# The opening of an encoder layer: 1/rms spread without a diagonal, chunk 0 by halves, the last squares summed apart, sums of h behind plain weights

## Chip, core and metric

The kernel runs on one core of a Trainium2 chip. The metric is the device time of one execution, in microseconds (us), as the median of several runs. TensorE (PE, with its weight loads PEld), VectorE (DVE), ScalarE (ACT), GpSimd (POOL) and SyncE (SP) run their own queues and wait for each other by semaphores; SP, ACT and POOL also issue DMAs.

## The reference

One layer on x (512 tokens, 1024 columns), all in float32, conditioned by a vector c:

```
mod = silu(c) @ w_mod + b_mod            # nine vectors: shift, scale, gate for three blocks
h = rmsnorm(x, norm_ffn1) * (1 + sc1) + sh1
x = x + 0.5 * g1 * swiglu(h, w_ffn1_in, w_ffn1_out)
h = rmsnorm(x, norm_mix) * (1 + sc2) + sh2
x = x + g2 * (merged(window attention, differential attention of h @ w_in) @ w_out)
h = rmsnorm(x, norm_ffn2) * (1 + sc3) + sh3
x = x + 0.5 * g3 * swiglu(h, w_ffn2_in, w_ffn2_out)
```

`rmsnorm(x, g)` is `x / sqrt(mean(x*x) + 1e-6) * g`, and `swiglu` is `(silu(gate) * up) @ w_out` with 2816 hidden columns.

## The kernel before

x lies transposed: 8 chunks of 128 model columns on the partitions, 512 tokens along the row. Products are made from two float32r parts of each operand, a high part (a cast on ACT, L185) and a low part (the difference on DVE, L186), as three products: high by high, high by low, low by high (`mm3`, L173 to L176).

**The opening** (from L606) is written out in the order in which each engine runs it (`manual_schedule`). c is loaded as one row and spread over the partitions by two products with a row of ones (L609); ACT takes SiLU of it into `cact`. While x arrives, ACT squares each chunk (DVE one of them, chunk 5), DVE adds the squares up, and PE sums them over the partitions with a column of ones (`Norm.sums`, L337), which leaves the sum for token t on partition t. DVE scales it (L307), POOL takes the power -0.5 (L308). To bring 1/rms of the tokens from the partitions onto the row of every partition, DVE multiplies the identity with it into a diagonal (`diagonal`, L316) and PE multiplies ones by that diagonal into a PSUM bank (`spread`, L329). `warm` (L615) puts products of the identity into PE's queue in between; their result is not used.

Then the 8 chunks follow. Of each chunk's scale and shift vectors DVE makes the column by multiplying a 128 x 1024 slice of w_mod with `cact` and summing the row (`mod_col`, L272), and for the scale a second, one-column operation applies the norm's gain (L279). `hidden` (L342) then makes h of the chunk: DVE x * scale * 1/rms (L346), ACT adds the shift into the high part (L347) and once more into a copy `value` (L350), DVE the low part (L351). PE multiplies the chunk by a 128 x 768 slice of weights, 18 products of 512 tokens into six banks (L689): three pairs of gate and up columns (q = 0, 1, 2). The weights' low parts are made by DVE for even chunks (L639), and for odd chunks by a negation on ACT (L632) and an adding DMA from POOL (L633). SP loads w_mod into the six slots of the tile `u` (4096 bytes a partition each) and weights into the four slots of `raw`; a load waits until its slot is free, and SP issues in order.

**The plain tiles** (from L835) come next, q = 3, 4, 5: each takes two loads of 128 x 1024 weights, splits them into parts and makes 48 products. `finish` (L723) reads a tile's pair of banks: SiLU on ACT (L725), the product on DVE (L726), and a split. Here PE, DVE and ACT are ordered by the scheduler of the tile framework, by its own cost model, with what is written first preferred; SP and POOL are in the order written. So DVE and ACT instructions of this part may stand ahead of instructions of the opening in their queue. **The sums of h** (`h_sum`, L587) subtract copies of h (L574, L576) and split the result into the operands n1, n2, t3, t4, which the later units of the first FFN multiply (a Strassen-like scheme: `Unit`, `two`, L444 to L446, 256 tokens each); n1 lies in slots of `u`. The first of them is read after q = 5.

Two **boundaries** later in the kernel (`boundary` at L360, and the one before the second FFN from L1752 on) repeat the norm on halves of the tokens (`HALVES`, T1 and T2), with `close`, `diagonal` and `spread` placed by step numbers among PE's products.

The pool lays out SBUF tile by tile in the order of first use, all slots of a tile side by side: the small tiles, ones, ident, then u (first used for c's row), par, x, the high and low parts with small columns between, ka, b, raw, f.

Of the kernel before, what the change touches and what calls it, by code (L numbers as in the profile page):

```python
# [11 lines left out]
F32 = mybir.dt.float32  # L12
# [122 lines left out]
def layer(ctx: ExitStack, tc: tile.TileContext, a: dict):  # L135
# [48 lines left out]
    def split_from(hi, lo, src):  # L184
        S.copy(hi, src)  # L185
        V.tensor_tensor(lo, src, f(hi), ALU.subtract)  # L186


    turn, holders = [0], {}

# [75 lines left out]

    def mod_col(v, c, w=None, in_order=False):
# [4 lines left out]
        ins = V.tensor_tensor_reduce(  # L272
            out=w, in0=w, in1=cact[0], scale=by, scalar=0.0 if v in norms else b, op0=ALU.mult, op1=ALU.add,
            accum_out=t,
        )
        if in_order:
            tc.keep_in_program_order(ins)
        if v in norms:
            V.scalar_tensor_tensor(t, t, par[:, norms[v] + c : norms[v] + c + 1], b, ALU.mult, ALU.add)  # L279

    class Norm:
# [28 lines left out]

        def diagonal(self, rs, r=FULL[0]):

            n = r.stop - r.start
            nt = n // P
            diag = f2()[:, 0:n]
            V.tensor_tensor(  # L316
                diag.rearrange("p (t q) -> p t q", t=nt),
                ident.unsqueeze(1).broadcast_to([P, nt, P]),
                rs.unsqueeze(2).broadcast_to([P, nt, P]),
                ALU.mult,  # L320
            )
            return diag

        def spread(self, diag, r=FULL[0]):

            n = r.stop - r.start
            rb = self.st[r.start] if n < T else bank("op")
            rb = rb[:, T - n : T]
            PE.matmul(rb, ones, diag, start=True, stop=True)  # L329
            return rb  # L330
# [11 lines left out]
    def hidden(rb, c, sc, sh, hi, lo, r=FULL[0], value=None):  # L342

        t = f2()[:, r]
        s = modv[sh][:, c : c + 1]
        V.scalar_tensor_tensor(t, x[c][:, r], modv[sc][:, c : c + 1], rb, ALU.mult, ALU.mult)  # L346
        S.activation(hi[:, r], t, AF.Identity, bias=s)  # L347
        yield
        if value is not None:
            S.activation(value, t.rearrange("p (t q) -> p t q", t=2), AF.Identity, bias=s)  # L350
        V.scalar_tensor_tensor(lo[:, r], t, s, f(hi[:, r]), ALU.add, ALU.subtract)  # L351
        yield
# [7 lines left out]
    def boundary(parts, g, norm, sc, sh, hh, hl, into, ahead, at):  # L360
# [29 lines left out]
        with tc.manual_schedule(engines=BOUND):  # L390
# [5 lines left out]
            for m, products in parts:  # L396
                po = bank("sc")[:, 0 : 2 * P]
                for _ in products(po, rb):
                    n += 1
                    if n == at[0]:  # L400
                        diag = norm.diagonal(norm.close(ra), ra)
                    elif n == at[1]:
                        ha = h_steps(norm.spread(diag, ra), ra)
                        run(ha, at[4])
# [5 lines left out]
            run(ha, at[6])  # L410
            diag = norm.diagonal(rs, rb)
            run(ha)
            run(steps, at[3])
            hb = h_steps(norm.spread(diag, rb), rb)
            run(hb)
# [189 lines left out]

    with tc.manual_schedule(engines=BOUND | {mybir.EngineType.SP, mybir.EngineType.Pool}):  # L606
        cb = [bank("sc") for i in range(2)]
        for i in range(2):
            PE.matmul(cb[i], ones[0:1, :], crow[:, i * T : (i + 1) * T], start=True, stop=True)  # L609

        def warm(n):

            out = bank("sc")[:, 0:P]
            for i in range(n):
                PE.matmul(out, ident, ident, start=True, stop=True)  # L615

        warm(8)
        w1 = {}

        def first_loads(k):  # L620
            scale = mod_load(SC1, k)
            raw = sbuf("raw", [P, 1024], F32, RAW)
            nc.sync.dma_start(raw[:, 0:768], a["w1s"][k])
            w1[k] = scale, mod_load(SH1, k), raw

# [19 lines left out]
        for c in range(NC):  # L645
            sq = f2()
            if c == 5:
                V.tensor_tensor(sq, x[c], x[c], ALU.mult)
            else:
                S.activation(sq, x[c], AF.Square)  # L650
            if c:
                V.tensor_tensor(sq, sq, before, ALU.add)
# [4 lines left out]
        n1.sums(sq, FULL[0], True, True)  # L657
        mod_col(SC1, 0, w1[0][0])
        rs = n1.rstd(FULL[0])
        warm(6)  # L660
        diag = n1.diagonal(rs)
        rb1 = n1.spread(diag)
        warm(5)
        mod_col(SH1, 0, w1[0][1])
        out1 = [b for _ in range(3) for b in pair_banks()]
        first_split(0)
        for k in range(NC):
            if k % 4 == 0:
# [3 lines left out]
                values = values.rearrange("p (t k q) -> p t k q", t=2, k=4)  # L672
            h1 = hidden(rb1, k, SC1, SH1, hh[k], hl[k], value=values[:, :, k % 4, :])
            next(h1)
            if k + 3 < NC:
                first_loads(k + 3)
            if k == 0:
                first_split(1)
                first_low(0)
            elif k + 1 < NC:  # L680
                mod_col(SC1, k + 1, w1[k + 1][0])
            next(h1)
            if k == 0:
                mod_col(SC1, 1, w1[1][0])
            wh, wl = w1.pop(k)[3:]
# [149 lines left out]
    with tc.manual_schedule(engines={mybir.EngineType.SP, mybir.EngineType.Pool}):  # L835
        for q in range(3):
            finish(q, out1[2 * q : 2 * q + 2])
        sums1 = ["n1", "n2", "t3", "t4"]
        units1 = {p: in_unit1(p) for p in range(PLAIN, NH)}
        for q in range(3, 2 * PLAIN):  # L840

            w = loaded1 or [load_split(a["w1i"][q - 3, k], aside=ASIDE * (q == 5)) for k in range(2)]
            loaded1 = None
            out = pair_banks()
            for k in range(NC):
                wh, wl = w[k // 4]
                for i in range(2):
                    o = (k % 4) * 256 + i * P
                    mm3(out[i], wh[:, o : o + P], wl[:, o : o + P], hh[k], hl[k], k == 0, k == NC - 1)
            for _ in range(2):  # L850
                if sums1:
                    h_sum(sums1.pop(0))
            finish(q, out)
            if q == 3:
# [890 lines left out]
    with tc.manual_schedule(engines=BOUND):  # L1745
# [28 lines left out]
        for q in ("a12", "a22"):  # L1774
            plain.prepare(q)
        diag = n3.diagonal(rs, T2)
        run(ha)
        lead.prepare("a12")
        run(steps, at[3])
        hb = h_steps(n3.spread(diag, T2), 1)  # L1780
        run(hb, 3)
# [95 lines left out]
def lay_out(i):  # L1877
# [4 lines left out]
    o["x"] = con(n["x"].reshape(T, NC, P).transpose(1, 2, 0))  # L1882
    o["c"] = n["c"].reshape(D)
    o["pos"] = con(n["positions"].reshape(NT, P).T)
# [54 lines left out]
```

## Time and profile before

| | us |
|---|---|
| median of 3 runs | 1062.57 |
| lowest and highest | 1062.09, 1063.57 |
| profiled execution, its own time | 1061.53 |
| its span, first to last instruction | 1059.8 |
| PE busy | 1040.5 |
| DVE busy | 794.8 |
| ACT busy | 566.2 |

In the rows of the timeline a start and a duration in us come first, then engine, line, operation, what is written and read by tile name, the count of merged instructions, and in brackets the idle time before and what ended it. A group's row has its busy time, the mean of one in ns, and the idle time before. A float32 product shows as two records, a float32r product as one; records of products that follow each other overlap.

### The profile page before, as it was taken

To read this page: it belongs to the slowest core of one execution; us is meant where nothing else is said; L and a number is where in the kernel's file an instruction comes from. 1 tells how busy PE (TensorE), PEld (TensorE's weight loads), DVE (VectorE), ACT (ScalarE), POOL (GpSimd) and SP (SyncE) were. 2 spreads that over 40 slices of the span, in tenths; PEclk is the share of its full clock that TensorE was granted. 3 is DMA by queue.
4 is the path that set the end of the run, shared out by engine and by line. 5 is a ranking of instruction groups with operands and counts; after the bars stand their busy time and mean duration, and the time that the engine had idled before them with its cause. 6 is when DMAs were issued, how large, how long until landed. Compare 5 with 4: busy or idle time off the path is not lost.

```text
span 1059.8 us, 18652 instructions
## 1 busy us (share of the span) xinstructions
PE 1040.5 (98%) x7316; PEld 952.6 (90%) x7316; DVE 794.8 (75%) x1459; ACT 566.2 (53%) x928; POOL 154.9 (15%) x174
## 2 busy tenths in 40 slices
PE   7999999999999999999999999999999999999998
PEld 5789889899899998899778778989999999999997
DVE  7985667667796679859773587977889787867867
ACT  5564334344454352667765755534766546655553
POOL 1100010100110100443211101001111211112210
PEclk9999999999999999999999999999999999999999
DMA  9968687966974459695747843975498998988974
GB/s 340 365 208 201 209 212 190 265 158 203 281 184 152 165 199 410 217 269 126 180 92 186 225 148 101 371 224 118 97 232 195 222 230 215 222 221 214 214 151 125
DMA packets 69082, 220.91 MB, mean 208 GB/s; under 512 B 8193, under 2 KB 10881, under 8 KB 68994
## 3 DMA queue, kind: packets, MB, share of 16 engines
q1 hardware_dynamic: 46512, 146.52, 38.6%
q0 software_dynamic: 19488, 68.70, 35.2%
q10 hardware_dynamic: 2994, 4.51, 1.2%
q8 instruction: 57, 0.93, 0.3%
q14 instruction: 31, 0.25, 0.1%
HBM read 209.46 MB, written 10.23 MB: 207 GB/s over the span
## 4 chain that ended last, share of the span: by engine, by line
PE 78%; DVE 8%; issue 5%; ACT 5%; DMA 2%; POOL 1%; SPq 0%; ACTq 0%; DVEq 0%; POOLq 0%
PE acc L446 5%; PE acc L444 5%; PE acc L445 5%; PE sc L174 5%; PE sc L446 5%; PE sc L444 5%; PE sc L175 5%; PE sc L445 5%; PE sc L176 5%; PE acc L174 4%; PE acc L175 4%; PE acc L176 4%; PE acc L1045 2%; PE acc L1047 2%; PE acc L1046 2%
## 5 line engine op out<-in xcount | busy, mean ns | idle before, releaser
L185 ACT CAST high<-raw 128x1024 fp32r<-128x1024 f32 (+2 forms) x162 | 158.3, 986 | 166.6 <-PE acc L445 39.1
L186 DVE TENSOR_TENSOR low<-raw,high 128x1024 fp32r<-128x1024 f32 (+2 forms) x162 | 183.6, 1141 | 59.4 <-ACT high L185 58.5
L444 PE MATMUL acc<-b,high 128*128 128x256 f32 x508 | 141.0, 278 | 0.3 <-DVE f L523 0.3
L445 PE MATMUL acc<-b,high 128*128 128x256 f32 x508 | 140.6, 277 | 0.1
L446 PE MATMUL acc<-b,low 128*128 128x256 f32 x508 | 140.6, 277 | 0.0
L444 PE MATMUL sc<-b,high 128*128 128x256 f32 x500 | 138.4, 277 | 1.4 <-ACT f L521 1.4
L446 PE MATMUL sc<-b,low 128*128 128x256 f32 x500 | 138.5, 277 | 0.0
L445 PE MATMUL sc<-b,high 128*128 128x256 f32 x500 | 138.4, 277 | 0.0
L186 DVE TENSOR_TENSOR low<-u,high 128x1024 fp32r<-128x1024 f32 (+1 forms) x73 | 87.5, 1200 | 27.6 <-ACT high L185 26.2
L185 ACT CAST high<-u 128x1024 fp32r<-128x1024 f32 (+1 forms) x73 | 75.5, 1035 | 54.8 <-PE sc L175 16.0
L174 PE MATMUL sc<-b,high 128*128 128x512 f32 (+1 forms) x280 | 100.8, 360 | 0.0
L175 PE MATMUL sc<-b,high 128*128 128x512 f32 (+1 forms) x280 | 100.3, 358 | 0.0
L176 PE MATMUL sc<-b,low 128*128 128x512 f32 (+1 forms) x280 | 100.2, 358 | 0.0
L444 PEld LDWEIGHTS acc<-b,high 128*128 128x128 f32 x508 | 95.4, 188 | 0.8 <-DVE f L523 0.5
L445 PEld LDWEIGHTS acc<-b,high 128*128 128x128 f32 x508 | 95.5, 188 | 0.4 <-DVE b L1727 0.3
L446 PEld LDWEIGHTS acc<-b,low 128*128 128x128 f32 x508 | 95.4, 188 | 0.2 <-DVE low L186 0.2
L444 PEld LDWEIGHTS sc<-b,high 128*128 128x128 f32 x500 | 94.0, 188 | 1.6 <-ACT f L521 1.6
L446 PEld LDWEIGHTS sc<-b,low 128*128 128x128 f32 x500 | 93.9, 188 | 0.3 <-DVE low L186 0.2
L445 PEld LDWEIGHTS sc<-b,high 128*128 128x128 f32 x500 | 93.9, 188 | 0.0
L174 PE MATMUL acc<-b,high 128*128 128x512 f32 (+1 forms) x248 | 92.1, 371 | 0.2 <-DVE u L186 0.2
L176 PE MATMUL acc<-b,low 128*128 128x512 f32 (+1 forms) x248 | 90.2, 364 | 0.0
L175 PE MATMUL acc<-b,high 128*128 128x512 f32 (+1 forms) x248 | 90.1, 363 | 0.0
(369 smaller groups left out, 2675.4 us busy)
## 6 DMA issues: line engine op xcount, KB each, us to landing
u<-w_mod SPq DMA_DIRECT2D x40, 512.0 KB, 7.8
b<-w_mod SPq DMA_DIRECT2D x32, 512.0 KB, 6.0
raw<-w2i SPq DMA_DIRECT2D x31, 512.0 KB, 5.5
u<-w2i POOLq DMA_DIRECT2D x31, 512.0 KB, 7.0
u<-w1u POOLq DMA_DIRECT2D x24, 512.0 KB, 7.1
raw<-w1u SPq DMA_DIRECT2D x24, 512.0 KB, 6.8
raw<-w1o SPq DMA_DIRECT2D x24, 384.0 KB, 4.2
raw<-w_gate SPq DMA_DIRECT2D x16, 512.0 KB, 5.6
```

Source lines behind the costliest of these rows:

```text
L174: PE.matmul(out, wh, xh, start=first, stop=False)
L175: PE.matmul(out, wh, xl, start=False, stop=False)
L176: PE.matmul(out, wl, xh, start=False, stop=last)
L185: S.copy(hi, src)
L186: V.tensor_tensor(lo, src, f(hi), ALU.subtract)
L444: PE.matmul(out, wh[:, s], xh, start=first and j == 0, stop=False, skip_group_check=True)
L445: PE.matmul(out, wh[:, s], xl, start=False, stop=False, skip_group_check=True)
L446: PE.matmul(out, wl[:, s], xh, start=False, stop=last and j == 1, skip_group_check=True)
L1045: PE.matmul(out[t][:, 0:n], hh[k][:, ht], wh[:, o : o + n], start=k == 0, stop=False)
L1046: PE.matmul(out[t][:, 0:n], hh[k][:, ht], wl[:, o : o + n], start=False, stop=False)
L1047: PE.matmul(out[t][:, 0:n], hl[k][:, ht], wh[:, o : o + n], start=False, stop=k == NC - 1)
```

## The change

It has six parts.

1. 1/rms is spread by products of its column, broadcast along the row as the stationary operand, with the identity as the moving one, 128 tokens each; `diagonal` goes, here and at both boundaries. c is loaded as eight columns and spread in the same way, so it takes a slot of the small tiles and none of u.
2. All squares are made on ACT. The sum runs over the first seven, and the last one is summed over the partitions by products of its own.
3. Chunk 0's h is made in two halves of 256 tokens.
4. The one-column operation for the scale (L279) moves from DVE to ACT for chunks 1 to 7. For chunk 0 the shift's slice is loaded ahead of the weights, and its column is made ahead of the spread.
5. The warm-up products are placed anew, some with chunks of x as the moving operand.
6. The next plain tile's loads and splits are written out ahead of the products of the one before, each behind the splits before them; the sums of h and `finish` are held behind splits of plain weights (`issue_after`), and all of n2, t3, t4 come with q = 5.

As u is now used first after b, its slots lie behind b's; every other tile keeps its place within 4096 bytes.

```diff
     def split_from(hi, lo, src):
-        S.copy(hi, src)
-        V.tensor_tensor(lo, src, f(hi), ALU.subtract)
+        last = S.copy(hi, src), V.tensor_tensor(lo, src, f(hi), ALU.subtract)
+        split[:] = [i.ins for i in last]
...
-    crow = u4(F32).rearrange("p a b -> p (a b)")[0:1, :]
-    nc.scalar.dma_start(crow, a["c"].unsqueeze(0))
+    ccol = small(NC)
+    nc.scalar.dma_start(ccol, a["c"])
...
         if v in norms:
-            V.scalar_tensor_tensor(t, t, par[:, norms[v] + c : norms[v] + c + 1], b, ALU.mult, ALU.add)
+            if beside:
+                S.activation(t, t, AF.Identity, bias=b, scale=par[:, norms[v] + c : norms[v] + c + 1])
+            else:
+                V.scalar_tensor_tensor(t, t, par[:, norms[v] + c : norms[v] + c + 1], b, ALU.mult, ALU.add)
...
-        def spread(self, diag, r=FULL[0]):
+        def spread(self, rs, r=FULL[0]):
...
-            PE.matmul(rb, ones, diag, start=True, stop=True)
+            for t in range(n // P):
+                PE.matmul(
+                    rb[:, t * P : (t + 1) * P], rs[:, t : t + 1].broadcast_to([P, P]), ident,
+                    start=t == 0, stop=(t + 1) * P == n, skip_group_check=True,
+                )
...
+        warm(4)
         cb = [bank("sc") for i in range(2)]
-        for i in range(2):
-            PE.matmul(cb[i], ones[0:1, :], crow[:, i * T : (i + 1) * T], start=True, stop=True)
...
-        warm(8)
+        for n in range(NC):
+            i, j = n // 4, n % 4
+            PE.matmul(
+                cb[i][:, j * P : (j + 1) * P], ccol[:, n : n + 1].broadcast_to([P, P]), ident,
+                start=j == 0, stop=j == 3, skip_group_check=True,
+            )
+        warm(5)
...
             sq = f2()
-            if c == 5:
-                V.tensor_tensor(sq, x[c], x[c], ALU.mult)
-            else:
-                S.activation(sq, x[c], AF.Square)
-            if c:
+            S.activation(sq, x[c], AF.Square)
+            if c == NC - 1:
+                last = sq
+            elif c:
                 V.tensor_tensor(sq, sq, before, ALU.add)
...
+                warm(4, x[c + 1])
+            elif c > 4:
+                warm(3, x[c])
+            if c == NC - 2:
+                n1.sums(sq, FULL[0], True, False)
+        n1.sums(last, FULL[0], False, True)
         mod_col(SC1, 0, w1[0][0])
         rs = n1.rstd(FULL[0])
-        warm(6)
-        diag = n1.diagonal(rs)
-        rb1 = n1.spread(diag)
         warm(5)
         mod_col(SH1, 0, w1[0][1])
+        rb1 = n1.spread(rs)
+        warm(4)
...
+            if k == 0:
+                h1 = [
+                    hidden(rb1, k, SC1, SH1, hh[k], hl[k], r, values[:, i : i + 1, k, :]) for i, r in enumerate(HALVES)
+                ]
...
-                mod_col(SC1, k + 1, w1[k + 1][0])
-            next(h1)
+                mod_col(SC1, k + 1, w1[k + 1][0], beside=True)
+            for h in h1:
+                next(h)
...
-            w = loaded1 or [load_split(a["w1i"][q - 3, k], aside=ASIDE * (q == 5)) for k in range(2)]
-            loaded1 = None
+            w, sums_from = loaded1, split[1]
+            if q < 5:
+                with tc.issue_after(split[0]), tc.issue_after(split[1]):
+                    loaded1 = [load_split(a["w1i"][q - 2, k], aside=ASIDE * (q == 4)) for k in range(2)]
+            behind = split[1]
...
-            for _ in range(2):
-                if sums1:
-                    h_sum(sums1.pop(0))
-            finish(q, out)
+            if q != 4:
+                with tc.issue_after(sums_from):
+                    for t in ("n1",) if q == 3 else ("n2", "t3", "t4"):
+                        h_sum(t)
+            with tc.issue_after(behind):
+                finish(q, out)
...
-                diag = n3.diagonal(n3.close(T1), T1)
+                rsa = n3.close(T1)
             elif i == len(last) - 1:
                 run(steps, at[1])
-                ha = h_steps(n3.spread(diag, T1), 0)
+                ha = h_steps(n3.spread(rsa, T1), 0)
```

On the host, c is laid out as 128 rows of 8 instead of one row of 1024.

More of the change, by code (lines that the diff above doesn't have):

```diff
@@ L349, in hidden @@
         if value is not None:
-            S.activation(value, t.rearrange("p (t q) -> p t q", t=2), AF.Identity, bias=s)
+            if r.stop - r.start == T:
+                t3 = t.rearrange("p (t q) -> p t q", t=2)
+            else:
+                t3 = t.unsqueeze(1)
+            S.activation(value, t3, AF.Identity, bias=s)
         V.scalar_tensor_tensor(lo[:, r], t, s, f(hi[:, r]), ALU.add, ALU.subtract)
@@ L606, in layer, with warm @@
     with tc.manual_schedule(engines=BOUND | {mybir.EngineType.SP, mybir.EngineType.Pool}):
-        cb = [bank("sc") for i in range(2)]
-        for i in range(2):
-            PE.matmul(cb[i], ones[0:1, :], crow[:, i * T : (i + 1) * T], start=True, stop=True)
[L611 to L615, printed above, removed]
-        warm(8)
+        fill = bank("acc")[:, 0:P]
+        def warm(n, by=ident):
+            for i in range(n):
+                PE.matmul(fill, ident, by[:, 0:P], start=True, stop=True)
+        warm(4)
+        cb = [bank("sc") for i in range(2)]
+        for n in range(NC):
[5 more added lines that the diff above has]
+        warm(5)
         w1 = {}
```

45 lines of the change are left out of this document (18 added, 27 removed).

## The prediction

> **What bounds the kernel now.** The page first, for the engine that fills the span, then the busy time by stretches of 10 us, then the order of time in the stretch where that engine is not full.
>
> ```profile
> span 1059.8 us, 18652 instructions
> PE 1040.5 (98%) x7316; PEld 952.6 (90%) x7316; DVE 794.8 (75%) x1459; ACT 566.2 (53%) x928; POOL 154.9 (15%) x174
> ```
>
> PE is the bound, with 19 us idle, and even those 98% hold warm-up products. So the time can fall in two ways: useful products begin sooner or follow each other without holes, or a product takes less.
>
> ```profile
> 10.00:20.00 10.00, 7.37 (x39) 6.19 (x38) 8.03 (x14) 3.16 (x5) 1.04 (x1) 0.83 1.03 411
> 20.00:30.00 10.00, 8.31 (x36) 6.19 (x35) 9.93 (x19) 6.51 (x10) 1.79 (x2) 1.00 1.01 346
> 30.00:40.00 10.00, 9.87 (x43) 7.70 (x42) 9.96 (x18) 5.55 (x8) 0.86 (x1) 1.00 1.04 373
> 40.00:50.00 10.00, 9.38 (x39) 6.77 (x38) 10.00 (x18) 4.65 (x7) 1.71 (x2) 1.00 1.05 356
> 50.00:60.00 10.00, 10.00 (x46) 8.25 (x45) 9.90 (x17) 8.08 (x14) 0.00 (x0) 1.00 0.94 291
> ```
>
> Columns: PE, PEld, DVE, ACT, POOL busy, granted clock, DMA share, GB/s. From 20 to 50 DVE is full and PE is not; but DMA is full too, from 10 to 50. That second saturation decides how much of a DVE saving can be cashed. From 50 on PE is full. Now the head of the stretch in order of time:
>
> ```profile
> 9.17 1.26 ACT L650 ACTIVATE f<-x 128x512 f32<-128x512 f32 x2 [0.58 <-DMA x<-x]
> 9.95 2.28 DVE L652 TENSOR_TENSOR f<-f,f 128x512 f32<-128x512 f32 x3
> 12.29 1.09 PE L337 MATMUL tp<-ones,f 128*128 128x2 f32 x8 [2.15 <-DVE f L652]
> 13.79 1.04 POOL L308 TENSOR_TENSOR sm<-sm,half 128x4 f32<-128x4 f32 x1 [4.75 <-DVE sm L307]
> 14.86 0.69 DVE L316 TENSOR_TENSOR f<-ident,sm 128x512 f32<-128x512 f32 x1 [1.16 <-POOL sm L308]
> 15.94 1.35 PE L329 MATMUL op<-f,ones 128*128 128x512 f32 x2
> 17.32 0.75 DVE L346 SCALAR_TENSOR_TENSOR f<-x,mod,op 128x512 f32<-128x512 f32 x1 [0.57 <-PE op L329]
> 18.88 0.50 PE L689 MATMUL acc<-b,high 128*128 128x512 f32 x1 [0.48 <-ACT b L347]
> 54.28 0.39 PE L689 MATMUL acc<-b,high 128*128 128x512 f32 x1
> ...
> 56.09 0.39 PE L174 MATMUL acc<-b,high 128*128 128x512 f32 x1
> ```
>
> The 144 products of L689 (8 chunks of 18) run from 18.88 until the plain tile q=3 begins at 56.09: 37.2 us. Between the last two rows lie 8 starts in 1.81 us, 0.227 each, so 144 need 32.7. The opening is 18.9 us of waiting and 4.5 us of holes. That is the store from which most parts of the change can draw.
>
> **The change part by part.** *Last squares apart.* Squares 6 and 7 wait for x (9.17), so they end at 10.4 as before. Adds shrink from three after 9.95 to two that can begin at 9.4 (square 5 is now ACT's), spacing 0.80, so the sum of seven ends near 10.9 instead of 12.2. But PE then has the sums of seven (8 records, 1.09), three warm-ups queued behind x[7] (6 records of about 0.11) and the sums of the last square: 10.95 + 0.9 + 0.7 + 1.1 = 13.6, against 13.4 now. I put this at 0; the ends are -0.7 (warm-ups not in the way) and +1.0 (if the clock is low).
>
> *Spread without a diagonal.* L316 goes: from POOL's end at 14.83 PE starts at once, 4 products of 2 records. The clock row says 0.83 for 10 to 20, so the two records of 1.35 us were partly at the low clock; 8 records of 0.11 to 0.21 plus 0.16 of drain are 1.05 to 1.85. At the high clock, which denser warm-ups should hold, the spread ends at 15.9, L346 starts at 15.95 instead of 17.32: -1.4 (at the low clock -0.6).
>
> *Chunk 0 by halves.* Two multiply-adds and two activations on 256 columns, where a pair on 512 took 1.56 (17.32 to 18.88); half-size ones overlap, so the first product is about 0.1 sooner: near 17.4, -1.5. DVE pays about 0.4 for four short instructions and for waiting on the activations before the low parts (an estimate), so chunk 1 gains only 1.0.
>
> *DVE's rounds.* In this stretch:
>
> ```profile
> L272 DVE CUSTOM_DVE_ANT_0 u<-u,ka,par 128x1024 f32<-128x1024 f32 x7 | 8.9, 1277 | 0.0
> L279 DVE SCALAR_TENSOR_TENSOR mod<-mod,par,begin 128x1 f32<-128x1 f32 x7 | 1.5, 214 | 0.1
> L576 DVE TENSOR_TENSOR b<-b 128x512 f32<-128x512 f32 x2 | 1.4, 684 | 0.0
> L186 DVE TENSOR_TENSOR u<-b,u 128x512 fp32r<-128x512 f32 x2 | 1.4, 684 | 0.0
> ```
>
> L279 moves to ACT (7 x 0.21), the sums of h (2 x L576, 2 x L186) leave the stretch: 1.5 + 2.8 = 4.3 us of DVE in the rounds, about the 4.5 us of holes. On ACT the small activation stands ahead of the copy of h, of the next cast of a weight and of its negation, whose POOL transfer waits for it; ACT is busy 5 to 6 of 10 us there, and the wait for L272 (1.2) falls where it now idles. I cost it at 0; without that cover up to 0.3 a round. The shift for chunk 0 is issued one load sooner and the first weight one later (some 1.3 us, to 13.4); its cast (0.8) still ends before 15.9. The column load of c has 128 short rows instead of 1 and its 8 products against ident may leave SiLU late; that sits behind the x that squares 6 and 7 wait for (9.17), and up to 0.5 us of it is hidden there.
>
> *What is late next: loads.* DVE would now let PE run unbroken from chunk 1, but odd chunks take their low weights by transfer:
>
> ```profile
> 28.01 0.50 PE L689 MATMUL acc<-b,low 128*128 128x512 f32 x1 [1.30 <-DMA low<-w1s]
> 34.65 0.84 ACT L630 CAST high<-raw 128x768 fp32r<-128x768 f32 x1 [1.21 <-DMA raw<-w1s]
> 36.52 0.86 POOL L633 DMA_DIRECT2D low<-w1s  x1 [9.63 <-ACT low L632]
> low<-w1s POOLq DMA_DIRECT2D x4, 384.0 KB, 7.8
> raw<-w1i SPq DMA_DIRECT2D x6, 512.0 KB, 9.1
> ```
>
> Chunk 1's transfer is issued some 1.4 sooner, as the activations ahead of its negation on ACT end that much sooner, and releases PE near 26.5 instead of 28.0. Unbroken PE would then want chunk 5's low part at 26.5 + 6 x 0.227 + (3 x 18 + 12) x 0.227 = 42.9. Its raw weight is DMA-bound (ACT waited for it at 34.65), and 36.52 + 7.8 = 44.3 is where it lands now. With DMA full before and after, a sooner request buys at most what idles; I take 43.4, between 42.4 and 44.3. After it PE has 6 + 36 products: 43.4 + 9.5 + 0.1 = 53.0. The opening ends 3.0 us sooner (2.0 to 4.0); losing the early start to a low clock would not change this end, since the loads set it.
>
> *Sums behind plain weights.* Work moves past PE's full stretch from 50 on, where only the due time counts: n1 by the first unit after q=5, the others 8 us later, with the casts of q=4 and q=5 now written out ahead of the products of the tile before. On SP the two w1i loads of the next tile now stand ahead of the first unit's load and a column's load, which are due 30 us later; POOL's adding transfer for that unit follows them and has the same room. I cost all this at 0, and its bad end is the last rival.
>
> *The moved tile.* c no longer takes a slot of u before everything else, so the pool lays the six slots of u behind b: they began 32 bytes off the 64-byte grid on which b, high and low lie, and come to lie on it. PE's groups by tile:
>
> ```profile
> L445 PE MATMUL sc<-b,high 128*128 128x256 f32 x500 | 138.4, 277 | 0.0
> L445 PE MATMUL sc<-u,high 128*128 128x256 f32 x72 | 20.1, 280 | 0.0
> L444 PE MATMUL acc<-u,high x80: 277/279/281, 100.1 to 1006.1; 128*128 128x256 f32 x80
> L174 PE MATMUL acc<-b,u 128*128 128x256 f32 x48 | 13.7, 286 | 0.0
> ```
>
> The same operation takes 277 ns in the mean with b moving and 280 with u. These records overlap, and a product that is 3 ns longer holds up the next by as much. (80 + 72) x 3 lines = 456 products x 3 ns = 1.4 us gained; 48 x 3 = 144 with u as weights (and b moving) may lose as much each, 0.4. I take -1.0, between -1.8 (456 x 4 ns, from 281, the longest of a row, to 277) and +0.4 (only the loss is real). The Trainium skill speaks against this term: SBUF — State Buffer, "Who interferes with whom", says that PE never waits on any other reader, and TensorE: Matmul & The Clock Gate, "Part 2: What happens when you issue a matmul", that loading weights takes no read bandwidth from the running product. By these an address changes nothing and the sum is 1.0 smaller; the rows above differ by tile, so I keep the term.
>
> *Later boundaries.* The diagonal also goes at both boundaries:
>
> ```profile
> 738.17 2.36 DVE L186 TENSOR_TENSOR low<-raw,high 128x1024 fp32r<-128x1024 f32 x2 [1.18 <-ACT high L185]
> 740.45 0.42 DVE L316 TENSOR_TENSOR f<-ident,sm 128x256 f32<-128x256 f32 x1
> 740.92 0.70 PE L329 MATMUL op<-f,ones 128*128 128x256 f32 x2 [0.50 <-DVE f L316]
> ```
>
> Here it stood behind two low parts and PE waited 0.5 for it. PE then waits again for DVE's next low part, which comes 0.3 sooner: -0.3 (0 to -0.5). Elsewhere PE does not wait for a diagonal.
>
> Sum: -3.0 - 1.0 - 0.3 = -4.3 us. The profiled execution took 1061.5 (span 1059.8), 1.0 below the median of 1062.57, so 1057.2 for it and 1058.3 for the median; the ends give -6.3 to -1.6.
>
> **The rivals.** *The address is worth nothing*: 1062.57 - 3.3 = 1059.3. For: 3 ns are 1% of a record whose end is modelled, and slot and bank differ between the groups too; against: it differs at the same line, with the same form, to the same bank.
>
> *The gain is given back to a load in the first FFN.*
>
> ```profile
> 172.45 1.05 ACT L185 CAST high<-raw 128x1024 fp32r<-128x1024 f32 x1 [3.82 <-DMA raw<-w1u]
> 140.00:150.00 10.00, 10.00 (x50) 8.40 (x49) 6.04 (x9) 1.05 (x1) 0.87 (x1) 1.00 0.60 193
> 150.00:160.00 10.00, 10.00 (x90) 10.00 (x88) 6.40 (x7) 6.02 (x7) 1.72 (x2) 1.00 1.04 292
> ```
>
> ACT stands 3.8 us for this load, with the copy that frees PE's bank behind it, and DMA is full (1.04) from 150 to 160. If the load keeps its time, the stall swallows the opening's 3.0: 1062.57 - 1.3 = 1061.3. Against: DMA is at 0.60 before 150, so the requests are released by engines, which come sooner too.
>
> *Casts of q=4 ahead of the finishing of q=0 (slower).* The load splits are now written out early; if ACT's order puts both casts before the SiLU that frees q=3's banks, PE at q=3 waits for a load.
>
> ```profile
> 44.13 2.11 SPq L211 DMA_DIRECT2D raw<-w1i  x2
> L725 ACT ACTIVATE f<-acc 128x512 f32<-128x512 f32 x3 | 1.6, 599 | 0.9 <-PE acc L689 0.9
> L726 DVE TENSOR_TENSOR f<-f,sc 128x512 f32<-128x512 f32 x3 | 1.9, 682 | 0.1
> ```
>
> The second request at 45.9 lands at 45.9 + 9.1 = 55.0; cast, SiLU, product: 55.0 + 1.05 (the cast at 172.45) + 0.6 + 0.7 + 0.5 for the handoffs between the two engines (an estimate) = 57.9, 1.8 after today's 56.09: 1062.57 + 1.8 - 1.3 = 1063.1 (a little slower); with DVE's two low parts (2.4) ahead of the product as well, 1065.5. It decides once that load lands after 51.0 or so. Against: the loads now go out ahead of others on SP, and the finishing of q=0 is written out first.
>
> **How the numbers follow.** Forecast 0.66, address worthless 0.12, swallowed 0.12, slower order 0.10. A change of under 0.2% (2.1 us) can't be told from none. Faster: 0.63 of the forecast's 0.66, 0.10 of the second; slower: half of the last and a little: 0.73, 0.20, 0.07. The forecast's own range is 1056.3 to 1061.0; to hold 8 in 10 with both later cases, 1055.6 to 1062.6.
>
> **What would show it.** Right: first L689 near 17.4, L174 of q=3 near 53.0, PE's longest hole in between before a low part by transfer and none before L347; no L576 in the rounds; u and b moving at one mean; PE's wait at the second boundary's spread gone; the clock at 1.00 from 13 to 17. Wrong: q=3 starting after 55, a hole between 53 and 90, or the stall near 174 longer by the same amount.

## The result, and the profile after

The changed kernel takes 1081.84 us (median of 6 runs, 1077.55 to 1083.53) against 1063.94 for the kernel before in the same series: a ratio of 1.0162, 95% interval 1.0137 to 1.0187. That is 17.9 us slower. The forecast was 1058.3, with 1055.6 to 1062.6 as its range.

The profiled execution of after took 1083.53 us (span 1081.6, before 1059.8), which is 22.0 more than the profiled one of before; the medians lie 17.9 apart. The head of its page:

```profile
span 1081.6 us, 18770 instructions
PE 1061.4 (98%) x7374; PEld 975.8 (90%) x7374; DVE 792.0 (73%) x1447; ACT 570.3 (53%) x938; POOL 156.1 (14%) x174
```

PE's busy time grew by 20.9 us and its idle time by only 0.9, though the change gives it only 58 records more, all of them small. So most of the loss is not waiting: PE takes longer over the same products. To find where, take the same product in both traces and subtract its start before from its start after:

| the product that starts before at | 60 | 120 | 160 | 180 | 240 | 320 | 500 | 540 | 740 | 760 | 860 | 960 | 1040 |
|---|---|---|---|---|---|---|---|---|---|---|---|---|---|
| after is later by, us | 0.6 | 1.4 | 1.6 | 0.5 | 1.4 | 3.0 | 3.5 | 11.3 | 11.4 | 12.6 | 15.6 | 19.0 | 21.8 |

There are two slow rises, one in each FFN (60 to 340 and 760 to 1040), and one leap between 500 and 540, in the attention, of which the diff touches no line. The 1.2 between 740 and 760 come with a stretch of half clock (755.8 to 759.2 in the clock's record). The opening gives 0.6 of loss instead of 3.0 of gain.

*The rises.* Busy time by stretches of 50 us in the second FFN, first before, then after (the count behind PE is that of its products):

```profile
800.00:850.00 50.00, 50.00 (x443) 50.00 (x442) 40.98 (x62) 30.80 (x48) 9.62 (x11) 1.00 0.91 210
850.00:900.00 50.00, 50.00 (x441) 50.00 (x440) 37.90 (x56) 27.67 (x40) 9.57 (x11) 1.00 0.92 223
```

```profile
800.00:850.00 50.00, 50.00 (x427) 50.00 (x426) 43.66 (x69) 31.51 (x52) 8.70 (x10) 1.00 0.88 212
850.00:900.00 50.00, 50.00 (x427) 50.00 (x426) 36.29 (x50) 24.58 (x32) 8.72 (x10) 1.00 0.91 213
```

PE is full and its clock 1.00 in all four rows, but it gets through 427 products where it got through 442. The groups by tile say of which kind they are, after:

```profile
L445 PE MATMUL sc<-b,high x500: 276/281/281, 92.6 to 1076.6; 128*128 128x256 f32 x167
L444 PE MATMUL acc<-u,high x80: 281/281/281, 100.9 to 1026.7; 128*128 128x256 f32 x80
```

and the first of these before:

```profile
L445 PE MATMUL sc<-b,high x500: 276/276/287, 92.0 to 1054.9; 128*128 128x256 f32 x167
```

(shortest, median and longest record in ns.) The median product with b moving went from 276 to 281. Those with u moving, which the change put on the 64-byte grid, did not fall to 276: they stand at 281, as against 279 before. One unit item of 24 products with u moving and the 120 products with b behind it, before and after, by windows cut at their first products:

```profile
100.06:102.86 2.80, 2.80 (x26) 2.80 (x25) 2.80 (x4) 1.73 (x3) 0.00 (x0) 1.00 1.01 349
102.86:116.48 13.62, 13.62 (x123) 13.62 (x121) 8.60 (x14) 6.18 (x9) 0.00 (x0) 1.00 0.40 126
```

```profile
100.94:103.76 2.82, 2.82 (x26) 2.82 (x25) 2.67 (x4) 2.82 (x5) 0.00 (x0) 1.00 0.77 236
103.76:117.89 14.13, 14.13 (x122) 14.13 (x121) 10.07 (x15) 6.29 (x10) 0.86 (x1) 1.00 0.51 133
```

The counts include a product or two carried over from ahead of the cut. Start to start, u's 24 take 2.80 and 2.82 us, the same. The 120 behind them take 13.62 (113.5 ns each) before and 14.13 (117.8) after, though operands, weights, banks and lines are the same and lie at the same offsets modulo 4096. From the start times one sees two paces and hardly anything between them: 113.3 ns and 117.8. Of the units' products with b moving (the b products) 92% (first FFN) and 88% (second) are under 115.5 ns before, 5% and 6% after. The pace hardly depends on what DVE or ACT do beside it: grouped by the instruction that runs there, the means after lie between 117.0 and 117.8 in every group of 50 products or more.

*The leap.* The chain of waits in the attention, after (start, us, what), and the stretch from 530 to 540 by windows, before and after:

```profile
525.11 0.96 ACT low L1005
526.07 0.46 issue
526.53 8.23 DMA low<-w_gate
534.80 0.79 PE acc L176
```

```profile
530.00:540.00 10.00, 9.58 (x65) 7.77 (x64) 7.15 (x20) 7.01 (x19) 1.71 (x2) 1.00 0.58 131
```

```profile
530.00:540.00 10.00, 5.57 (x14) 4.12 (x13) 3.56 (x12) 4.01 (x13) 1.96 (x2) 0.70 0.72 145
```

PE waits 4.4 us for a gate's low part, and the granted clock drops behind the wait (0.70 in the mean; half from 533.9 to 540.8 in the clock's record), which costs another 3.4. That transfer is not later than the rest of the stage, as its issue before and after shows:

```profile
522.87 0.91 POOL L986 DMA_DIRECT2D low<-w_gate  x1 [6.30 <-ACT low L985]
```

```profile
526.53 0.91 POOL L1006 DMA_DIRECT2D low<-w_gate  x1 [6.47 <-ACT low L1005]
```

It goes out 3.66 us later, where all else is 3.5 later. The instructions are those of before, but PE's order in this stage is another one, and it comes to this gate's products sooner.

*The opening*, in order of time:

```profile
8.63 0.60 ACT L661 ACTIVATE ka<-sc 128x512 f32<-128x512 f32 x1 [0.93 <-PE sc L618]
9.12 2.18 ACT L653 ACTIVATE f<-x 128x512 f32<-128x512 f32 x4
9.78 2.28 DVE L657 TENSOR_TENSOR f<-f,f 128x512 f32<-128x512 f32 x3 [2.00 <-ACT f L653]
14.85 1.27 DVE L273 CUSTOM_DVE_ANT_0 u<-u,ka,par 128x1024 f32<-128x1024 f32 x1
15.03 2.00 POOL L312 TENSOR_TENSOR sm<-sm,half 128x4 f32<-128x4 f32 x1 [4.82 <-DVE sm L311]
17.08 1.83 PE L321 MATMUL op<-ident,sm 128*128 128x128 f32 x8 [0.46 <-POOL sm L312]
20.43 0.50 PE L705 MATMUL acc<-b,high 128*128 128x512 f32 x1 [0.62 <-ACT b L344]
55.18 0.50 PE L705 MATMUL acc<-b,low 128*128 128x512 f32 x1 [1.05 <-DMA low<-w1s]
56.67 0.39 PE L174 MATMUL acc<-b,high 128*128 128x512 f32 x1
```

The first product comes at 20.43 (18.88 before), and q = 3 at 56.67 (56.09). ACT's second SiLU waits 0.93 for the column's products, with four squares behind it; the power on POOL takes 2.00 where it took 1.04; the spread runs at half clock (15.1 to 18.5 in the clock's record; before has half clock from 13.2 to 16.6); and the last wait ahead of q = 3 is for chunk 7's low part.

### The profile page after: what moved, and what is told of

Same layout as the page of the kernel before. It is cut to its first block, busy times and chain, and to the rows that moved or that the text cites. A ratio compares the mean times of both kernels' runs of the same rounds, so it can differ in the third digit from the quotient of the medians.

```text
span 1081.6 us, 18770 instructions
## 1 busy us (share of the span) xinstructions
PE 1061.4 (98%) x7374; PEld 975.8 (90%) x7374; DVE 792.0 (73%) x1447; ACT 570.3 (53%) x938; POOL 156.1 (14%) x174
## 4 chain that ended last, share of the span: by engine, by line
PE 74%; issue 9%; DVE 6%; DMA 5%; ACT 4%; POOL 2%; ACTq 0%; DVEq 0%; POOLq 0%; SPq 0%
PE sc L445 5%; PE sc L446 5%; PE sc L444 5%; PE sc L174 5%; PE sc L176 5%; PE sc L175 5%; PE acc L446 5%; PE acc L445 5%; PE acc L444 5%; PE acc L176 4%; PE acc L174 4%; PE acc L175 4%; PE acc L1065 2%; PE acc L1067 2%; PE acc L1066 2%
## 5 line engine op out<-in xcount | busy, mean ns | idle before, releaser
L444 PE MATMUL acc<-b,high 128*128 128x256 f32 x508 | 143.4, 282 | 0.1
L445 PE MATMUL acc<-b,high 128*128 128x256 f32 x508 | 143.1, 282 | 0.2 <-DVE b L1747 0.2
L446 PE MATMUL acc<-b,low 128*128 128x256 f32 x508 | 143.1, 282 | 0.1
L444 PE MATMUL sc<-b,high 128*128 128x256 f32 x500 | 140.4, 281 | 0.0
L445 PE MATMUL sc<-b,high 128*128 128x256 f32 x500 | 140.4, 281 | 0.0
L444 PEld LDWEIGHTS acc<-b,high 128*128 128x128 f32 x508 | 97.2, 191 | 0.6 <-DVE f L523 0.3
L445 PEld LDWEIGHTS acc<-b,high 128*128 128x128 f32 x508 | 96.5, 190 | 0.5 <-DVE b L1747 0.4
```

Source lines behind the costliest of these rows:

```text
L444: PE.matmul(out, wh[:, s], xh, start=first and j == 0, stop=False, skip_group_check=True)
L445: PE.matmul(out, wh[:, s], xl, start=False, stop=False, skip_group_check=True)
L446: PE.matmul(out, wl[:, s], xh, start=False, stop=last and j == 1, skip_group_check=True)
```

## The experiments

**Is it the tile?** The theory, called the pace theory: PE has two paces that last, and products whose moving operand lies off the grid leave it in the faster one. Before the change, u's items did that once or more in each unit. Rivals: where high, low and b lie (the change moved them down by 24,576 bytes), and the new order of instructions.

`e1_tile_back`, the changed kernel with one line more:

```diff
+    u4(F32)
     ccol = small(NC)
```

> The changed kernel, but the six slots of u lie where they lay before (an unused first slot is asked for ahead of par), so u begins 32 bytes off the 64-byte grid again and x, high, low and b get their old addresses back; not one instruction differs. Pace theory: a product of 256 columns has two paces that last, 113.3 and 117.8 ns, and products whose moving operand lies off the grid leave PE in the fast one. Then b-moving products of the units run at 113 to 114 ns in both FFNs, which gives back 4.3 us in the first and 9.3 us in the second: 1081.8 - 13.6 = about 1068. The wait for a low part in the attention (4.4 us at 530, and 6.8 us at half clock behind it) stays, since PE's order there stays. Place theory (where high, low and b lie in the memory sets the pace): the same 1068. Order theory (the loss comes from the new order of instructions): about 1081, products at 117.8 ns.

Measured 1069.64 (ratio 1.0062, 1.0043 to 1.0081): 1.00% of the change's 1.62%, or 10.6 us, come back. b products at 113.8 and 114.0 ns, 89% and 85% of them under 115.5. Aligned with before, it is 0.0 at 60, -0.2 at 500, 6.4 at 540 and 6.0 at 1040: both rises are gone, the leap is whole. Order of instructions is out for the rises.

`e2_only_tile_moved`, before with c by columns alone (the diff's parts `ccol`, its eight products and the host's layout):

> The kernel before with one part of the change: c is loaded as a column and spread by 8 products, so it needs no slot of u, and u comes to lie behind b, on the grid; all else is as before, the diagonal too. Pace theory and place theory: the unit products go at 117.8 ns nearly throughout, 4.3 + 9.3 us lost: about 1077.5; no wait of 4.4 us in the attention. Order theory: about 1064.

Measured 1075.94 (1.0118, 1.0101 to 1.0135), b products at 117.5 and 117.6 ns. 2.5 us of its profile are the opening: PE begins the sums of squares at 13.55 instead of 12.29, behind the column's late SiLU, and then runs at half clock for 6.8 us (13.7 to 20.6) where before does for 3.4.

`e12_on_grid_in_place`, before, u moved by 32 bytes where it lies, and all that follows it by 128:

```diff
+    pos = keep([P, NT], "pos", I32)
     crow = u4(F32).rearrange("p a b -> p (a b)")[0:1, :]
...
+    posf = keep([P, NT], "posf")
+    keep([P, 16], "pad")
     par = keep([P, NPAR], "par")
```

> The kernel before, with the instructions of before, where u is moved by 32 bytes and nothing else of note: pos stands ahead of u, posf and an unused tile behind it, so u begins on the 64-byte grid and all that follows lies 128 bytes further. Pace theory: b-moving unit products at 117.5 ns, 4.3 + 9.3 us lost: 1076. Place theory: 113.8 ns and 1063.

Measured 1074.57 (1.0109, 1.0090 to 1.0129); b products at 117.4 and 117.6 ns. Its second FFN by windows:

```profile
850.00:900.00 50.00, 50.00 (x427) 50.00 (x427) 38.19 (x55) 25.12 (x35) 8.68 (x10) 1.00 0.94 225
900.00:950.00 50.00, 50.00 (x427) 50.00 (x426) 37.26 (x58) 30.96 (x49) 8.74 (x10) 1.00 0.82 191
```

427 again, with the instructions of before: moving u by 32 bytes cost 1.09%, or 11.6 us. Aligned with before, its profile is 1.5 us later at 60 (its sums of squares took 1.86 us, 1.09 before), 4.1 at 340 and at 740, and 13.4 at 1040: both rises, 2.6 and 9.3 us, and no leap. That the 128 bytes play no part is not tried by itself; in `e3` and `e11` below u moves while high, low and b stay.

`e3_32_bytes` and `e11_96_bytes`, the changed kernel with u behind b, but off the grid:

```diff
     hh, hl = new_h()
+    keep([P, 8], "pad")
```

> The changed kernel with one unused tile of 32 bytes ahead of u: u stays behind b but begins 32 bytes off the grid; high, low, b and x stay where the change put them. Pace theory: the units at 113 to 114 ns, about 1068, as with the tile put back. Place theory: 117.8 ns and about 1081.8. Order theory: about 1081.8.

Measured 1074.58 (1.0105, 1.0088 to 1.0123), between the two theories: b products at 114.8 and 114.9 ns, 69% and 66% under 115.5. Its windows, cut as above (24 with u, 72 with b, 24 with u, 120 with b):

```profile
89.81:92.65 2.84, 2.84 (x26) 2.84 (x25) 2.84 (x5) 2.22 (x4) 0.86 (x1) 1.00 0.73 111
92.65:101.13 8.48, 8.48 (x74) 8.48 (x73) 5.06 (x8) 2.99 (x4) 0.00 (x0) 1.00 0.90 265
101.13:103.97 2.84, 2.84 (x26) 2.84 (x25) 2.62 (x4) 2.84 (x5) 0.00 (x0) 1.00 0.61 171
103.97:117.60 13.63, 13.63 (x122) 13.63 (x121) 9.91 (x15) 6.33 (x10) 0.86 (x1) 1.00 0.52 134
```

The first u item leaves PE in the slower pace (8.48 / 72 = 117.8), the second in the faster (13.63 / 120 = 113.6). Here u begins at 96 modulo 128, before it was 32. So with 96 bytes instead of 32:

> The changed kernel with 96 bytes ahead of u instead of the 32 of e3 (pos moved there, and an unused tile of 64 bytes): u lies behind b as the change put it, and begins at 32 modulo 128, as in the kernel before, where e3 had 96. If the offset modulo 128 decides in which pace off-grid products leave PE: b-moving unit products 113.8 ns, nearly 90% of them fast as with the tile put back, about 1069.6. If the place of u, high, low and b decides the rest: 114.9 ns, two thirds fast, as in e3, 1074.6.

Measured 1069.48 (1.0061, 1.0042 to 1.0081), as with the tile put back; 88% of the second FFN's b products under 115.5 (113.9 ns), 73% of the first's. The first FFN alone does not tell e11 from e3 (69%), but 74% is also what `e7` below has there, with u where it was before. Counted by items with u moving, in both FFNs: they leave PE in the faster pace 23 times of 24 before, 22 in e1 and in e11, 13 in e3, and never in after, e2 and e12. So among offsets off the grid the one modulo 128 decides, not the place.

`e4_two_off_grid`, the changed kernel with two products off the grid ahead of each s1 item (the one with u moving):

```diff
+            if q == "s1" and new and self.operand in (h1_operand, h_operand):
+                for _ in range(2):
+                    PE.matmul(po[:, 0:H], self.ready[q][0][:, 0:P], h_op["n1"][0][:, 0, 8 : 8 + H], ...)
```

> The changed kernel, u on the grid, with two more products ahead of every unit's s1 item (18 items, 36 products, 4.2 us by 0.118 each), whose moving operand is the same tile read from 32 bytes further; their result is overwritten. Pace theory: they leave PE in the fast pace, so s1 items and all that follows run at 113.3: 1081.8 - 13.6 - 1.9 (s1 items: 18 x 24 x 4.4 ns) + 4.2 = about 1070.5. If two products are too few to change the pace, and by the place and the order theory: about 1086, products at 117.8.

Measured 1085.54 (1.0212, 1.0196 to 1.0227), b products at 117.1 and 117.6 ns: 0.5% more than after, or 5 us, where 4.2 were worked out for the 36 products. Two did not change the pace (one item of 24 left PE in the faster one). But these two read from 32 bytes behind u's place, which is 96 modulo 128 as in e3, where items of 24 succeed only in part; two at 32 modulo 128, and how many it takes, were not tried.

**What makes the leap?** In the traces, the order of PE's 863 records from the attention's first transpose to its last, which the scheduler lays, is that of before in every variant with the old loop over q = 3, 4, 5, and that of after in every variant with the new one, whatever else is undone (at most 8 records stand elsewhere within each kind, 55 to 66 between the two). One run for each side:

`e5_sums_as_before`, e1 with the loop of before:

> The changed kernel with the tile put back, and the loop over q = 3, 4, 5 (splits of w1i and the sums of h) as it was before; the rest of the change stays. Reorder theory: the written-out sums make the scheduler lay PE's order in the attention differently, though no line there is changed, so that gate products stand ahead of their low part; with the old loop the old order returns, the wait of 4.1 us near 527 and the 6.8 us at half clock behind it go: 1069.6 - 6.2 = 1063.4. Opening theory (the opening's other times shift everything and so the wait): the wait stays, about 1069.

`e6_sums_alone`, before with the loop of after:

> The kernel before with one part of the change: the sums of h and the splits of w1i held behind plain weights; u stays where it was. Reorder theory: the wait for low<-w_gate of some 4 us and the half clock behind it appear near 527: 1063 + 6.2 = 1069, less up to 1.1 if the wait near 174 goes with it. Opening theory: 1062 to 1063.

e5 took 1062.22 against 1062.32 (1.0000, 0.9989 to 1.0011), e6 1068.59 (1.0061, 1.0044 to 1.0077). The opening theory falls on both sides: the new loop alone brings the wait, the old one takes it away. PE's wait in e6, and the stretch from 530 to 540 in e5:

```profile
530.36 0.79 PE L176 MATMUL acc<-b,low 128*128 128x512 f32 x1 [3.77 <-DMA low<-w_gate]
```

```profile
530.00:540.00 10.00, 9.57 (x62) 7.36 (x58) 7.91 (x22) 7.35 (x21) 0.93 (x1) 1.00 0.54 107
```

The two effects taken alone (e12 and e6) cost 1.09% and 0.61%, together 1.70% of the time; the whole change cost 1.62%. All that is left of it (e5) is worth nothing that can be measured. By which of its estimates the scheduler swaps those products is open.

**Where did the opening's gain go?** From e5 on, one obstacle after another was taken away.

`e7_column_ahead`:

```diff
+        mod_col(SH1, 0, w1[0][1])
         rs = n1.rstd(FULL[0])
         warm(5)
-        mod_col(SH1, 0, w1[0][1])
```

> As e5_sums_as_before, but the column of the shift for chunk 0 (1.27 us of VectorE) stands ahead of rstd, where VectorE idles 1.3 us, instead of beside GpSimd's power. Port theory: the power took 2.0 us after the change (1.04 before) because it runs beside this column; it falls to 1.0, the spread starts 1.0 us sooner. What follows: if the opening's end is set by the order of work, q = 3 starts 1.0 sooner and the time is 1062.4; if the loads set it, q = 3 still starts near 56 and the time stays at 1063.4. Rival to the port theory: the power takes 2.0 us still.

Measured 1061.33 (0.9992, 0.9982 to 1.0002). The power on POOL, in e5 and then in e7:

```profile
14.96 2.00 POOL L313 TENSOR_TENSOR sm<-sm,half 128x4 f32<-128x4 f32 x1 [4.97 <-DVE sm L312]
```

```profile
15.20 1.04 POOL L313 TENSOR_TENSOR sm<-sm,half 128x4 f32<-128x4 f32 x1 [5.25 <-DVE sm L312]
18.96 0.50 PE L706 MATMUL acc<-b,high 128*128 128x512 f32 x1 [0.62 <-ACT b L345]
53.75 0.50 PE L706 MATMUL acc<-b,low 128*128 128x512 f32 x1 [0.98 <-DMA low<-w1s]
```

The port theory holds: the power is 0.96 us shorter when DVE does not run the column beside it. q = 3 starts at 55.24, where it started at 56.41 in e5: the end of the opening moves with the order of work, although PE still waits 0.98 for chunk 7's transfer.

`e8_row_of_c`, e7 with c as a row again:

> As e7_column_ahead, and c is a row again (a short transfer, two products of ones by the row), without the column's 8 products. The column made SiLU's second half wait for PE (0.93 us) with squares 4 to 7 behind it. So squares end 0.9 sooner and the first product of chunk 0 is near 18.0 (19.9 with the tile put back). If the order of work sets the opening's end: 1061.5; if the loads do: 1063 to 1063.4, q = 3 near 56.

Measured 1061.77 (0.9989, 0.9977 to 1.0002). The first product came at 19.12, not 18.0. Why, from its order of time:

```profile
7.08 3.40 PE L612 MATMUL acc<-ident 128*128 128x128 f32 x16
8.71 2.28 DVE L653 TENSOR_TENSOR f<-f,f 128x512 f32<-128x512 f32 x3 [0.44 <-ACT f L649]
10.32 2.40 PE L612 MATMUL acc<-x,ident 128*128 128x128 f32 x20
12.55 0.95 PE L332 MATMUL tp<-ones,f 128*128 128x2 f32 x8
```

The sum of seven squares is ready at 8.71 + 2.28 = 11.0, and PE comes to it at 12.55, behind 36 records of warm-up products. So taking the column away gains nothing by itself: PE began these sums at 12.39 in e7.

`e9_low7_by_vector`, e7 with one line changed:

```diff
-BY_DMA = (1, 3, 5, 7)
+BY_DMA = (1, 3, 5)
```

> As e7_column_ahead, and chunk 7's low part is made by VectorE instead of by a transfer (BY_DMA without 7). There PE waits 0.98 us at 52.8 for that transfer, issued at 44.9 and landing at 53.7 behind the loads of w1i. Loads theory: this transfer ends the opening; q = 3 starts at 54.3 instead of 55.3, time 1061.3 - 1.0 = 1060.3. VectorE theory (it is full from 20 to 50, so its 0.95 us come back as another wait): q = 3 at 55.3 or later, 1061.3 or more.

Measured 1061.27 against 1063.25: 0.9980 (0.9969 to 0.9991). q = 3 starts where it was expected, with the first product as late as before the change:

```profile
18.75 0.50 PE L706 MATMUL acc<-b,high 128*128 128x512 f32 x1 [0.62 <-ACT b L345]
```

```profile
54.28 0.39 PE L174 MATMUL acc<-b,high 128*128 128x512 f32 x1
```

That is 1.8 us sooner than before. The median did not come down to the 1060.3 expected: by their ratios e9 is 0.12% below e7, and the intervals overlap. And the 1.8 is of one execution at full clock; e10 below has the same opening, met half clock from 15.0 to 18.4, and began chunk 0 at 19.72 and q = 3 at 55.25, 0.97 later each. This version, e10 and e13 are those whose interval lies below 1.

`e13_no_warm_on_x`, e9 with c as a row and without the thirteen warm-ups on x:

> As e9_low7_by_vector, and what still stands ahead of the first product is taken away: c is a row again (as in e8) and the ten warm-up products on x ahead of the sums of squares and the three more between them are left out. In e8 the sum of seven squares was ready at 11.0, and PE came to it at 12.55 behind these warm-ups. So the sums end 1.5 to 2.0 us sooner and the first product of chunk 0 comes at 16.8 to 17.3 instead of 18.75, unless the half clock returns (then 17.5 to 18.2). Order theory: q = 3 then starts 1.5 sooner (at 52.8 instead of 54.3), time 1059.8. Loads theory: with VectorE and DMA full from 20 to 50, the gain is swallowed in holes of the rounds, q = 3 within 0.5 of 54.3, time 1060.8 to 1061.3.

Measured 1061.88 against 1063.11: 0.9983 (0.9970 to 0.9995). The profiled execution had half clock (13.4 to 16.8 in the clock's record), and the first product came at 18.20, 0.55 sooner than in e9, and q = 3 at 53.69, 0.59 sooner. Against e10, which met half clock too, both are 1.5 sooner: the order theory. Later waits in the first FFN, which e9's execution did not have, took it back, such as one of 1.09 for ACT at 306.9:

```profile
300.00:310.00 10.00, 8.91 (x77) 8.64 (x75) 9.50 (x21) 6.14 (x9) 0.86 (x1) 1.00 0.87 256
```

`e10_diagonal_back`, e9 with `diagonal` and the old `spread` at the two later boundaries alone:

> As e9_low7_by_vector, with the diagonal back at the two later boundaries alone. Without the diagonal VectorE's chain there is 0.33 shorter and PE's two waits are 0.76 each; 3.4 us of half clock began 1.5 us after them in four of the seven profiles so made (1.2 us lost, e5 and e8), in none of three with the diagonal. Clock theory: 0.34 lost, 1.2 to 1.5 won in about half of the executions: 0.3 to 0.5 faster than e9. No-clock theory: 0.3 slower than e9.

Measured 1061.46 (0.9987, 0.9978 to 0.9996), not to be told from e9. Across the second boundary e9's profile gained 0.26 and e10's lost 0.18; the half clock came in neither. Over all profiles it followed this boundary in 4 of 10 without the diagonal and in none of 5 with it, too few to call the diagonal the cause. The stretch from 740 to 750 in e5, where the half clock came, and in e7:

```profile
740.00:750.00 10.00, 8.48 (x58) 8.08 (x57) 6.76 (x14) 6.92 (x13) 0.59 (x1) 0.83 0.44 147
```

```profile
740.00:750.00 10.00, 8.49 (x70) 8.09 (x70) 6.77 (x13) 6.59 (x12) 0.00 (x0) 1.00 0.49 160
```

Same waits, 58 products against 70.

## Why the prediction was wrong, point by point

**The moved tile (-1.0): wrong in sign, and the largest miss.** The step that failed is "These records overlap, and a product that is 3 ns longer holds up the next by as much", applied to u's own 456 products as if the price sat on them. In its place e12 showed that u's products are no cheaper on the grid (117.8 ns start to start in the first FFN, against 117.0 off it), and that their offset sets the pace of the thousands of b products behind them: some 3,600 products by 3.7 ns are 13.3 us, of which 11.9 show in the two rises of e12's profile and 11.6 in the medians. The row that showed it was quoted, b at 277 and u at 280, but read as a property of the tile; the starts of the products behind each u item would have shown the pace change there. I also used two pages of the Trainium skill for "By these an address changes nothing" (SBUF — State Buffer, "Who interferes with whom", and TensorE: Matmul & The Clock Gate, "Part 2: What happens when you issue a matmul"). That was my inference: they speak of other readers and of weight loads, not of an operand's own offset, and against the inference stand 32 bytes and 1.09%.

**Sums behind plain weights (0): wrong.** The argument that "only the due time counts" looked at what the moved instructions wait for, and that part held. What it left out is that the attention's order is not written by hand: e6 shows the same edit shifting it, 0.61%.

**The opening (-3.0): wrong by 3.6 in the profile.** The forecast had the first product at 17.4 and q = 3 at 53.0, so 35.6 us between them, where before takes 37.2. In after the first product came 1.55 later than before, and 36.2 us lie behind it. Of the 1.55, the sums of squares end 1.23 later (DVE's next instruction at 14.77, before at 13.54) and the power is 0.96 longer; from its end to the first multiply-add it took 1.92 instead of 2.49, and the halves gave 0.08. Four steps failed.

1. The column's lateness was taken as hidden behind x ("up to 0.5 us of it is hidden there"). SiLU waited 0.93 with four squares behind it, and the sum of seven was ready at 12.06 (9.78 + 2.28), not at 10.9.
2. The column of the shift was counted as moved for free; it ran beside POOL's power and doubled it (e7). The Trainium skill has the rule (SBUF — State Buffer, "SBUF: two separate sides": VectorE and GpSimd share a pair of ports under an exclusive lock), and the trace agrees: 2.00 us beside the column, 1.04 without.
3. "At the high clock, which denser warm-ups should hold": the spread met half clock in after, as in e3 and e11, and full clock in e1, e4 and e5, all with the same opening. These warm-ups do not settle it.
4. The forecast held that "losing the early start to a low clock would not change this end, since the loads set it". The end moved with the start. e7 begins 1.47 sooner than after and reaches q = 3 1.43 sooner, though PE waits for a transfer in both (0.98 and 1.05), and that is chunk 7's, not chunk 5's; the w1i loads issued ahead of it on the same full DMA were in sight.

The step on DVE's 4.3 us was right: with chunk 7's transfer gone, 35.5 us lie between the first product and q = 3 in e9, e10 and e13, where 35.6 were forecast.

**Last squares apart (0, ends -0.7 and +1.0).** The 1.23 lie beyond the bad end. What follows the sum of seven took 2.7 us, as added up (0.9 + 0.7 + 1.1); the sum itself was late by the column. The warm-ups would have held it up too: in e8, without the column, PE came at 12.55 to a sum ready at 11.0, and e13, without both, began the sums at 10.81.

**The second boundary (-0.3): right in size.** e1 and e7 gain 0.34 across it. Not foreseen was the half clock behind it, which took 1.2 net in after, e3, e5 and e8.

**The rivals.** The stall near 174 did not grow but went, and after makes up 1.1 us between 160 and 180; PE is full there:

```profile
170.00:180.00 10.00, 10.00 (x87) 10.00 (x86) 7.36 (x10) 5.66 (x8) 0.86 (x1) 1.00 0.61 197
```

The casts of q = 4 did not block q = 3 either: PE is full from 60 to 100. My two slower mechanisms were both local, of 1 to 3 us; neither true one was among them, so the range missed by 19 us.

## What to carry to other kernels

When an edit moves a tile, by however few bytes, compare the start-to-start time of the products *behind* the tile's, not only its own: in a kernel in which PE is full, 4 ns on each product made two thirds of the loss (1.09% of 1.62%). An edit can cost its time in a stage that it doesn't touch, wherever the order there is laid by a scheduler, so compare the built order of every stage first. And when a chain of waits is shortened, ask for each stretch behind it whether it will start sooner or wait for something that does not move: here the end of the opening moved with its start.

## What the runs showed of the hardware

- Back-to-back products of 256 float32r columns, weights changing each time, kept one of two paces at full clock, 113.3 or 117.8 ns start to start, over hundreds of products. Items with the moving operand at 32 modulo 128 left PE in the faster pace 21 to 23 times of 24 in each of ten profiles (23 before, 22 in e1 and e11), at 96 in 13 (e3), on the 64-byte grid never (after, e2, e12). Other things change the pace too: before, it was the faster one ahead of the 144 products of 512 columns from 116.48 on, and the slower one behind them; and near 1064 in the profile of after, two products started 0.37 and 0.23 us behind those before them, and nearly all that follow, to the end, go at 113.3. What the paces come from was not settled.
- GpSimd's power on 128x4 took 2.00 us beside VectorE's multiply-and-sum over 1024 columns and 1.04 without it.
- Two waits of 0.76 to 0.87 us within 2 us were followed by 3.4 us of half clock in 4 of 10 profiles. That the waits are the cause was not shown.
- The same instructions of the opening met half clock in some executions and not in others: e9 did not, e10 did, and chunk 0 began 0.97 us later.
